# Hybrid SSD and differential-attention layer: the skip path moved into the attention stage, two kinds of DMA moved to ScalarE's queue

## The chip, the cores and the metric

The kernel runs on one core of a Trainium2 chip. The metric is the device time of one execution in microseconds (us). Three runs of the kernel before gave 1235.99, 1236.02 and 1239.23 us, median 1236.02 us. The trace comes from one further execution, under the hardware profiler.

Engines: PE is TensorE's matmul, PEld its weight load, DVE is VectorE, ACT ScalarE, POOL GpSimd, SP SyncE, which here only issues DMAs. Each engine works through its own queue in order.

## The reference, cut to what matters

One encoder layer on 1024 tokens of width 1024. The input is normalised once; that result feeds the layer and, scaled by alpha, also the skip sum at the end.

```python
h = layer_norm(x, ln_emb_g, ln_emb_b)
proj = h @ w_in                      # 1024 x 6688
z, xbc, dt_f, dt_b, q, k, v, g = split(proj)
xbc = silu(centred_dwconv(xbc, conv_w, conv_b))
y = bidirectional_ssd(xs, dt_f, dt_b, Bm, Cm, ...)      # 16 heads, chunks of 128
y_ssm = rms_norm(y * silu(z), ssm_norm_g)
# 8 heads, two softmax maps each, distance penalty
o = (softmax(q1 k1) - lam * softmax(q2 k2)) @ v
y_attn = rms_norm(o, subln_g) * (1 - lam_init) * silu(g)
mix = concat([y_ssm, y_attn]) @ w_out
return layer_norm(ALPHA * h + mix, ln_g, ln_b)
```

## The kernel before, in words

**Arithmetic.** Matmuls run in fp32r. To keep fp32 accuracy, each operand is split into a rounded high part and a low remainder, and a product takes three matmuls (high by high, high by low, low by high). The high part is a cast on ACT, the low part a subtraction on POOL or DVE.

**Stages.** (1) Up to about 60 us: x is loaded, normalised, transposed and split (`h_hi`, `h_lo`). (2) To about 434 us: 52 column blocks of `w_in` begin to be projected (the lane `fill`, weights staged by `weights` in tiles `wst`, split into `whi` and `wlo`), and the two SSD groups run beside them. (3) About 434 to 1085 us: attention, eight heads after each other, eight blocks of 128 queries each, 64 blocks in all. The remaining projections of the next head fill PE between the attention steps. (4) From about 975 us, overlapping the last head: the output projection by `w_out`, then the skip sum and the last layer norm, row block by row block.

**One attention block.** PE computes two score maps into `sc`. DVE adds the distance term and takes the row minimum (tiles `p`, one custom instruction each). ACT exponentiates each (`ACTIVATE p<-p,nm`). DVE forms the two reciprocals `rs`; POOL scales the first map (`TENSOR_SCALAR p<-p,rs`); DVE subtracts the scaled second map from it (`SCALAR_TENSOR_TENSOR p<-p,rs,p`). PE transposes the result (`bk<-ident,p`), ACT and DVE split the transposes into `wh` and `wl`, and PE multiplies by the values every second block. At most two blocks are between scores and transposes.

**What sets the order.** The lanes are Python generators. A planner (`Loom`, lines 47 to 127) emits them into the program in the order of a model of engine times; `LANES` (line 29) holds each lane's rank and margin. PE's instructions, and those issued through `VO` and `AO`, are pinned in that order. Everything else (most of DVE and ACT, all of POOL and SP) is ordered once more by the tile framework's scheduler when the program is built: it may move an instruction ahead of others of its engine if its data and its buffer allow it. On the chip, each engine runs the order that comes out of this.

**DMAs.** All are issued by SP (`dma`, line 250). An SP instruction that waits (for a buffer to be free or for data to be ready) holds up all that stand behind it. The z block's tail (line 478) stores the gated `zs` to DRAM in 16 pieces; `proj_k` (line 921) copies each half of the keys to the other 64 partitions, four DMAs a head. Every DMA's completion counts on one of eight semaphores, given out in turn.

**The skip path.** The lane `residuals` (lines 1189 to 1219) runs in stage 4, once the pool `ow` is open (line 1292). It loads the embedding gain and bias, broadcast to all partitions (`g_e`, `b_e`), scales both by alpha on ACT, and then, for each of the eight row blocks in two halves (tiles `xr`, 128 x 512): a load of x, the normalisation on ACT (line 1213), the multiplication by the gain and the addition of the bias on POOL. The output projection's accumulators (PSUM banks `bk`) are freed by DVE's addition of a bank to `xr` (lines 1225, 1280).

Of the kernel before, what the change touches and what calls it, by code (L numbers as in the profile page):

```python
# [9 lines left out]
F32 = mybir.dt.float32  # L10
# [4 lines left out]
ALU = mybir.AluOpType  # L15
# [10 lines left out]
EPS = 1e-5  # L26
ALPHA = 2.0 ** 0.25

LANES = dict(weights=(0, 0.8), channels=(1, 1.2), steps=(2, 1.6), z_tail=(2, 0.8), conv=(3, 1), v_tail=(3, 0.4), states=(4.4, 0.8), diag=(4.125, 0.6), maps=(4.4, 0.6), gate=(4.375, 0.2), finish=(4.2, 2), scores=(4, 0.8), combine=(4.125, 0.6), values=(4.25, 0.4), fill=(9, 0.8), rows_out=(9, 0.2), y_out=(9, 3), residuals=(9, 2), project_out=(9, 2))


def col_bcast(ap, n):
# [184 lines left out]
def hybrid_layer_kernel(  # L217
# [13 lines left out]
    VO = Engine(loom, nc.vector, "DVE", _dve_cost, pinned=True)  # L231
    AO = Engine(loom, nc.scalar, "ACT", _act_cost, pinned=True)
    SP = Engine(loom, nc.sync, "DMA", _dma_cost)
    x, out = x[0], out[0]
    w_in, w_out, conv_w = w_in[0], w_out[0], conv_w[0]

# [12 lines left out]

    def dma(dst, src):  # L250
        SP.dma_start(dst, src)

    def transpose(dst, src, n=128):
        T.transpose(dst, src, ident[:n, :n])
# [109 lines left out]
    y_dram = [dr.tile([128, 16, 128], F32, name=f"yd{k}") for k in range(8)]  # L364
    acs_dr = [dr.tile([16, NCH, 128], F32, name=f"acs_d{d}") for d in range(2)]
    zd = [dr.tile([NCH, 128, 512], F32, name=f"zd{g}") for g in range(2)]


    g0x = px.enter_context(ExitStack())
# [96 lines left out]
    def z_block(g, j, when=None):  # L466
        def evac(half, ps):
            zr = late["sq"].tile([128, 512], F32, name="zr", bufs=2)
            A.copy(zr, ps)

            def tail():
                pt = bank((128, 4, 128))
                yield (zr, pt)
                for i in range(4):
                    transpose(pt[:, i, :], zr[:, 128 * i:128 * i + 128])
                zs = late["sq"].tile([128, 4, 128], F32, name="zs", tag="zr", bufs=2)
                A.activation(zs, pt, AF.Silu)
                dma(zd[g][4 * half:4 * half + 4, :, 128 * j:128 * j + 128].rearrange("c p n -> p c n"), zs)
                G[g].z_done += 1
            loom.add(tail(), "z_tail")  # L480
        queue.append(Block(Z0 + 512 * g + 128 * j, evac, when))
# [427 lines left out]
    def proj_k(h):  # L909
        H = heads_[h]  # L910

        def evac(half, ps):
            if half == 0:
                H.kk = H.pool().tile([128, 2, S], F32R, name="kk")
                H.kl = H.pool().tile([128, S], F32R, name="kl")
            t = slice(512 * half, 512 * half + 512)
            for m in range(2):
                a, b = slice(64 * m, 64 * m + 64), slice(64 - 64 * m, 128 - 64 * m)
                A.copy(H.kk[a, m, t], ps[a])
                V.tensor_sub(H.kl[a, t], ps[a], H.kk[a, m, t].bitcast(F32))  # L920
                dma(H.kk[b, m, t].bitcast(F32), H.kk[a, m, t].bitcast(F32))
            H.k += 1
        queue.append(Block(K0 + 128 * h, evac, free_since(h, "scored", 8)))

# [176 lines left out]
    for h in range(1, 8):  # L1101
        project_head(h)
    queue[-2].pair = queue[-1].last = True
    for lane in (scores, combine, values):
        loom.add(lane())


# [74 lines left out]
                parts.append((hi, lo))  # L1182
            ahead[tb, part] = parts

    res = {}
    used = set()
    halves = [slice(0, 512), slice(512, 1024)]

    def residuals():

        yield lambda: "pool" in res
        for n, src in (("g", ln_emb_g), ("b", ln_emb_b)):
            res[n] = res["pool"].tile([128, D], F32, name=n + "_e")
            dma(res[n], src.partition_broadcast(128))
            A.activation(res[n], res[n], AF.Copy, scale=ALPHA)
        late = [("zr", 2), ("zr", 2), ("o", 2), ("o", 2), ("osq", 1), ("msq", 1)]
        for tb in range(8):
            yield lambda: tb < len(used) + 2 or tb > NE
            if tb == NE:
                yield lambda: last.v == 2  # L1200
            if tb > NE:
                yield lambda: last.done == 2
            xr = []
            nmr = ap.tile([128, 1], F32, name="nmr", bufs=2)
            V.scalar_tensor_tensor(nmr, mv[tb][:, 0:1], -1.0, rstd[tb], op0=ALU.mult, op1=ALU.mult)
            for n, t in enumerate(halves):
                if tb < NE:
                    xr.append(res["pool"].tile([128, 512], F32, name=f"xr{tb}_{n}"))
                else:
                    tag, bufs = late[2 * (tb - NE) + n]  # L1210
                    xr.append(ap.tile([128, 512], F32, name="xr", tag=tag, bufs=bufs))
                dma(xr[n], x[128 * tb:128 * tb + 128, t])
                A.activation(xr[n], xr[n], AF.Identity, scale=rstd[tb], bias=nmr)
                P.tensor_mul(xr[n], xr[n], res["g"][:, t])
                P.tensor_add(xr[n], xr[n], res["b"][:, t])
            res[tb] = xr
        for n, src in (("g", ln_g[0]), ("b", ln_b[0])):
            res[n + "o"] = res["pool"].tile([128, D], F32, name=n + "_o", tag=n + "_e")
            dma(res[n + "o"], src.partition_broadcast(128))

    def norm_out(tb, xr, po, final):
        st = ap.tile([128, 2, 6], F32, name="bst", bufs=2)
# [95 lines left out]
```

## Time and profile before

| | |
|---|---|
| median of three runs | 1236.02 us |
| the profiled execution | 1237.79 us |
| its span, first to last instruction | 1236.1 us |
| PE busy | 1177.5 us (95%) |
| DVE busy | 903.5 us (73%) |
| ACT busy | 702.8 us (57%) |
| POOL busy | 472.6 us (38%) |
| mean granted TensorE clock | 0.989 |

The shares are means over stages with different limits: PE's idle time, 58.6 us of the span, lies before 60 us (16.2 us of it), in the SSD stage, in some places of stage 4 and after 1200 us (7.7 us), and hardly any in the attention stage. So the rows below are taken stage by stage. A row of the timeline merges equal instructions that follow each other; in brackets stands the idle time of the engine before it and who ended it.

### The profile page before, as it was taken

To read this page: it belongs to the slowest core of one execution; us is meant where nothing else is said; L and a number is where in the kernel's file an instruction comes from. 1 tells how busy PE (TensorE), PEld (TensorE's weight loads), DVE (VectorE), ACT (ScalarE), POOL (GpSimd) and SP (SyncE) were. 2 spreads that over 40 slices of the span, in tenths; PEclk is the share of its full clock that TensorE was granted. 3 is DMA by queue.
4 is the path that set the end of the run, shared out by engine and by line. 5 is a ranking of instruction groups with operands and counts; after the bars stand their busy time and mean duration, and the time that the engine had idled before them with its cause. 6 is when DMAs were issued, how large, how long until landed. Compare 5 with 4: busy or idle time off the path is not lost. (4 is left out here: it accounts for less than half of the span.)

```text
span 1236.1 us, 16491 instructions
## 1 busy us (share of the span) xinstructions
PE 1177.5 (95%) x5881; PEld 923.5 (75%) x5881; DVE 903.5 (73%) x1303; ACT 702.8 (57%) x1281; POOL 472.6 (38%) x404
## 2 busy tenths in 40 slices
PE   5999999899989999999999999999999998999997
PEld 3777667788667777778787777878778776778885
DVE  6686876767875568788788887887878889952334
ACT  4557478734468456565655657556655686641221
POOL 7412564322753223323232333233232429541354
PEclk9999999999999999999999999999999999989999
DMA  6113236522345521011111121121111262233221
GB/s 198 34 32 116 81 110 173 181 65 53 99 118 149 151 63 43 26 46 50 26 48 39 43 53 26 34 52 36 43 36 42 86 225 83 74 103 114 77 86 60
DMA packets 107592, 98.04 MB, mean 79 GB/s; under 512 B 9364, under 2 KB 79349, under 8 KB 107509
## 3 DMA queue, kind: packets, MB, share of 16 engines
q1 hardware_dynamic: 107509, 96.98, 27.4%
q8 instruction: 46, 0.75, 0.3%
q14 instruction: 37, 0.30, 0.1%
HBM read 75.85 MB, written 16.91 MB: 75 GB/s over the span
## 5 line engine op out<-in xcount | busy, mean ns | idle before, releaser
L140 PE MATMUL bk<-hh,whi 128*128 128x512 f32 x832 | 353.8, 425 | 1.3 <-DVE yt L140 0.7
L140 PE MATMUL bk<-hl,whi 128*128 128x512 f32 x832 | 328.1, 394 | 3.3 <-POOL hl L140 3.0
L140 PE MATMUL bk<-hh,wlo 128*128 128x512 f32 x832 | 328.9, 395 | 0.0
L140 POOL TENSOR_TENSOR wlo<-wst,whi 128x512 fp32r<-128x512 f32 x104 | 160.4, 1546 | 145.1 <-ACT whi L140 129.0
L140 ACT ACTIVATE p<-p,nm 128x1024 f32<-128x1024 f32 x128 | 146.8, 1148 | 121.3 <-DVE nm L140 120.6
L140 POOL TENSOR_SCALAR p<-p,rs 128x1024 f32<-128x1024 f32 x56 | 64.5, 1152 | 350.1 <-DVE rs L140 300.4
L140 PEld LDWEIGHTS bk<-hh,whi 128*128 128x128 f32 x832 | 158.3, 190 | 33.8 <-issue 5.7
L140 PEld LDWEIGHTS bk<-hh,wlo 128*128 128x128 f32 x832 | 157.2, 189 | 35.3
L140 PEld LDWEIGHTS bk<-hl,whi 128*128 128x128 f32 x832 | 158.3, 190 | 33.2 <-POOL hl L140 5.5
L140 DVE CUSTOM_DVE_ANT_0 p<-sc,dist 128x1024 f32<-128x1024 f32 x128 | 151.3, 1217 | 11.9 <-PE sc L140 11.2
L140 DVE SCALAR_TENSOR_TENSOR p<-p,rs,p 128x1024 f32<-128x1024 f32 x64 | 127.8, 1997 | 22.6 <-POOL p L140 18.0
L140 DVE TENSOR_TENSOR wl<-bk,wh 128x512 fp32r<-128x512 f32 x128 | 86.9, 683 | 16.1 <-ACT wh L140 14.2
L140 ACT CAST wh<-bk 128x512 fp32r<-128x512 f32 x128 | 74.1, 579 | 43.1 <-PE bk L140 42.4
L140 ACT CAST whi<-wst 128x512 fp32r<-128x512 f32 x104 | 64.0, 621 | 44.4 <-PE bk L140 37.5
L140 PE MATMUL bk<-ident,p 128*128 128x128 f32 x512 | 79.9, 279 | 4.7 <-DVE wl L140 3.0
L140 PEld LDWEIGHTS bk<-ident,p 128*128 128x128 f32 x512 | 61.9, 142 | 29.5 <-DVE wl L140 6.5
L140 ACT ACT_TABLE_LOAD x46 | 59.0, 1283 | 27.9 <-DVE t L140 17.2
L140 PE MATMUL bk<-wh,vh 128*128 128x256 f32 x256 | 74.6, 291 | 0.0
L140 PE MATMUL bk<-wl,vh 128*128 128x256 f32 x256 | 72.2, 282 | 0.9 <-DVE wl L140 0.9
L140 PE MATMUL sc<-kk,q 128*128 128x512 f32 x256 | 72.4, 394 | 0.0
L140 PE MATMUL bk<-wh,vl 128*128 128x256 f32 x256 | 72.0, 281 | 0.0
L140 PEld LDWEIGHTS bk<-xt,t 128*128 128x128 f32 x256 | 44.9, 189 | 24.3 <-issue 15.8
(217 smaller groups left out, 2168.3 us busy)
## 6 DMA issues: line engine op xcount, KB each, us to landing
wst<-in_w_in_dram SPq DMA_DIRECT2D x104, 256.0 KB, 3.0
t<-acs_d SPq DMA_DIRECT2D x64, 256.0 KB, 3.4
ws<-in_w_out_dram SPq DMA_DIRECT2D x32, 256.0 KB, 3.1
ys<-yd SPq DMA_DIRECT2D x32, 256.0 KB, 3.1
xb<-in_x_dram SPq DMA_DIRECT2D x8, 512.0 KB, 6.3
zd<-zs SPq DMA_DIRECT2D x16, 256.0 KB, 3.0
gz<-zd SPq DMA_DIRECT2D x16, 256.0 KB, 3.1
yd<-ys SPq DMA_DIRECT2D x16, 256.0 KB, 2.5
```

Source lines behind the costliest of these rows:

```text
L140: r = f(*args, **kw)
```

## The change

Three edits go together.

(1) **A new lane `skip_rows`**, with rank 9 and margin 2 in `LANES`, starts with the attention lanes. It loads `g_e` and `b_e`, and for each of 16 half row blocks loads x into a tile `xe` (two buffers), normalises it on ACT, multiplies and adds on POOL, and stores it to DRAM (`xr_dram`). `residuals` then only loads `xr` from there. The last gain and bias (`g_o`, `b_o`) are loaded in `skip_rows` too.

(2) **`dma_act`**: the 16 z stores and the 32 key copies are issued by ACT in place of SP.

(3) The DMA scratch is set to 1024 bytes, which leaves room in SBUF for the new tiles.

```diff
+    AD = Engine(loom, nc.scalar, "DMA", _dma_cost)
...
+    def dma_act(dst, src):
+
+        AD.dma_start(dst, src)
...
+    xr_dram = [dr.tile([128, D], F32, name=f"xrd{b}") for b in range(NCH)]
...
-                dma(zd[g][4 * half:4 * half + 4, :, 128 * j:128 * j + 128].rearrange("c p n -> p c n"), zs)
+                dma_act(zd[g][4 * half:4 * half + 4, :, 128 * j:128 * j + 128].rearrange("c p n -> p c n"), zs)
...
-                dma(H.kk[b, m, t].bitcast(F32), H.kk[a, m, t].bitcast(F32))
+                dma_act(H.kk[b, m, t].bitcast(F32), H.kk[a, m, t].bitcast(F32))
...
-    for lane in (scores, combine, values):
+    resid = {}
+
+    def skip_rows():
+
+        for n, src in (("g", ln_emb_g), ("b", ln_emb_b)):
+            resid[n] = ap.tile([128, D], F32, name=n + "_e")
+            dma(resid[n], src.partition_broadcast(128))
+        yield lambda: count["s"] > 1
+        for n in "gb":
+            A.activation(resid[n], resid[n], AF.Copy, scale=ALPHA)
+        left = []
+
+        def store():
+            dst, t = left.pop(0)
+            dma(dst, t)
+
+        for i in range(16):
+            tb, t = i // 2, slice(512 * (i % 2), 512 * (i % 2) + 512)
+            yield lambda: count["s"] >= 3 * i + 3
+            if len(left) > 1:
+                store()
+            xe = ap.tile([128, 512], F32, name="xe", bufs=2)
+            dma(xe, x[128 * tb:128 * tb + 128, t])
+            nmr = ap.tile([128, 1], F32, name="nmr", bufs=2)
+            V.scalar_tensor_tensor(nmr, mv[tb][:, 0:1], -1.0, rstd[tb], op0=ALU.mult, op1=ALU.mult)
+            A.activation(xe, xe, AF.Identity, scale=rstd[tb], bias=nmr)
+            P.tensor_mul(xe, xe, resid["g"][:, t])
+            P.tensor_add(xe, xe, resid["b"][:, t])
+            left.append((xr_dram[tb][:, t], xe))
+        yield lambda: count["s"] >= 54
+        while left:
+            store()
+        for n, src in (("g", ln_g[0]), ("b", ln_b[0])):
+            res[n + "o"] = ap.tile([128, D], F32, name=n + "_o", tag=n + "_e")
+            dma(res[n + "o"], src.partition_broadcast(128))
+
+    res = {}
+    for lane in (scores, combine, values, skip_rows):
         loom.add(lane())
...
         yield lambda: "pool" in res
-        for n, src in (("g", ln_emb_g), ("b", ln_emb_b)):
-            res[n] = res["pool"].tile([128, D], F32, name=n + "_e")
-            dma(res[n], src.partition_broadcast(128))
-            A.activation(res[n], res[n], AF.Copy, scale=ALPHA)
...
-                dma(xr[n], x[128 * tb:128 * tb + 128, t])
-                A.activation(xr[n], xr[n], AF.Identity, scale=rstd[tb], bias=nmr)
-                P.tensor_mul(xr[n], xr[n], res["g"][:, t])
-                P.tensor_add(xr[n], xr[n], res["b"][:, t])
+                dma(xr[n], xr_dram[tb][:, t])
             res[tb] = xr
...
-    nc = _bacc.Bacc("TRN2", target_bir_lowering=False, num_devices=1)
+    nc = _bacc.Bacc("TRN2", target_bir_lowering=False, num_devices=1,
+                     dynamic_dma_scratch_size=1024)
```

PE's order is the same up to the last head and differs there in where the output projection's groups stand among the steps of attention. The orders of the other engines change where the new instructions go. The condition `count["s"] >= 3 * i + 3` spreads the 16 pieces over 48 blocks in the planner's order, but the built program has them in the first ten blocks of attention. The tiles `xe` are named below by their buffer numbers: the first to the last are 9200, 9207, 9215, 9223, 9231, 9239, 9247, 9255, 9263, 9271, 9279, 9287, 9295, 9303, 9311 and 9319; the text numbers them 0 to 15 and calls the blocks of attention b0, b1, and so on.

**POOL, from b3 to b4 of the first head.** `p0` is the first map of a block (p0_4001 and p0_4009 are b3, p0_4106 and p0_4114 are b4). Before:

```order
L140 TENSOR_SCALAR p0_4001<-p0_4001,rs_4069 128x1024
L140 TENSOR_TENSOR wlo_4151<-wst_4067,whi_4150 128x512
L140 TENSOR_SCALAR p0_4106<-p0_4106,rs_4177 128x1024
L140 TENSOR_SCALAR p0_4171<-p0_4171,rs_4246 128x1024
L140 TENSOR_TENSOR o_4011<-o_4011,gate_3823 128x512
```

and now:

```order
L140 TENSOR_SCALAR p0_4009<-p0_4009,rs_4077 128x1024
L140 TENSOR_TENSOR xe_9247<-xe_9247,g_e_9194 128x512
L140 TENSOR_TENSOR xe_9247<-xe_9247,b_e_9196 128x512
L140 TENSOR_TENSOR wlo_4159<-wst_4075,whi_4158 128x512
L140 TENSOR_TENSOR xe_9255<-xe_9255,g_e_9194 128x512
L140 TENSOR_TENSOR xe_9255<-xe_9255,b_e_9196 128x512
L140 TENSOR_TENSOR xe_9263<-xe_9263,g_e_9194 128x512
L140 TENSOR_TENSOR xe_9263<-xe_9263,b_e_9196 128x512
L140 TENSOR_SCALAR p0_4114<-p0_4114,rs_4185 128x1024
```

Between the scaling of b3 and that of b4, POOL now multiplies and adds three tiles `xe`.

**ACT, around the exponentials of b4 and b5 of the first head** (`ACTIVATE p0,ls` and `p1,ls`; p0_4106 and p0_4114 are b4, p0_4171 and p0_4179 b5). Before:

```order
L140 CAST wh_4039<-bk_4112 128x4x128
L140 ACTIVATE p0_4106,ls_4095<-p0_4106,nm_4094 128x1024
L140 ACTIVATE p1_4109,ls_4095<-p1_4109,nm_4094 128x1024
L140 CAST wh_4039<-bk_4125 128x4x128
L140 CAST kk_4134<-bk_4061 64x512 x2
L140 ACTIVATE p0_4171,ls_4156<-p0_4171,nm_4155 128x1024
```

and now:

```order
L140 CAST wh_4047<-bk_4120 128x4x128
L140 ACTIVATE xe_9263<-xe_9263,nmr_9265,rstd4_96 128x512
L140 ACTIVATE p0_4114,ls_4103<-p0_4114,nm_4102 128x1024
L140 ACTIVATE p1_4117,ls_4103<-p1_4117,nm_4102 128x1024
L140 CAST wh_4047<-bk_4133 128x4x128
L140 CAST kk_4142<-bk_4069 64x512
L140 ACTIVATE xe_9271<-xe_9271,nmr_9273,rstd4_96 128x512
L140 DMA kk_4142<-kk_4142 64x512
L140 CAST kk_4142<-bk_4069 64x512
L140 DMA kk_4142<-kk_4142 64x512
L140 ACTIVATE xe_9279<-xe_9279,nmr_9281,rstd5_97 128x512
L140 ACTIVATE p0_4179,ls_4164<-p0_4179,nm_4163 128x1024
```

Tile 8 (9263) stands ahead of b4's exponentials, tile 10 (9279) ahead of b5's, and the key copies stand in ACT's queue.

**SP, in the same stretch.** `wst` are weights of the projections, `xe<-in_x_dram` the loads and `xrd` the stores of the skip rows. Before:

```order
L140 DMA wst_4065<-in_w_in_dram 128x4x128
L140 DMA wst_4067<-in_w_in_dram 128x4x128
L140 DMA wst_4254<-in_w_in_dram 128x4x128
L140 DMA wst_4256<-in_w_in_dram 128x4x128
L140 DMA kk_4134<-kk_4134 64x512 x2
```

and now:

```order
L140 DMA xrd3_147<-xe_9247 128x512
L140 DMA wst_4264<-in_w_in_dram 128x4x128
L140 DMA xe_9263<-in_x_dram 128x512
L140 DMA xrd3_147<-xe_9255 128x512
L140 DMA xe_9271<-in_x_dram 128x512
L140 DMA xrd4_148<-xe_9263 128x512
L140 DMA xe_9279<-in_x_dram 128x512
L140 DMA xrd4_148<-xe_9271 128x512
L140 DMA xe_9287<-in_x_dram 128x512
```

With two buffers, each load of a tile waits for the end of the store that empties its buffer: 9263 for that of 9247, 9279 for that of 9263.

## Rows read from the trace of the kernel before

**Rows 1.** Busy time by stretch: length, PE, PEld, DVE, ACT, POOL, clock, DMA share, GB/s

```profile
600.00:800.00 200.00, 199.21 (x1072) 157.50 (x1071) 161.93 (x239) 122.69 (x213) 61.17 (x45) 1.00 0.16 40
...
```

**Rows 2.** The same view, in the last head and the last stage

```profile
1026.00:1036.00 10.00, 6.04 (x21) 4.90 (x22) 8.96 (x10) 9.16 (x15) 9.92 (x7) 0.83 0.23 71
...
1083.00:1092.00 9.00, 6.13 (x20) 4.73 (x19) 5.67 (x9) 5.04 (x9) 4.11 (x3) 0.64 0.34 106
...
```

**Rows 3.** Timeline of PE in the last head: start, us, instruction, idle time before

```profile
1029.96 0.51 PE L140 MATMUL bk<-oh,oyh 128*128 128x512 f32 x1 [3.98 <-DVE xr L140]
...
1032.26 1.20 PE L140 MATMUL bk<-oh,oyh 128*128 128x512 f32 x2
...
1035.11 0.62 PE L140 MATMUL bk<-ol,oyh 128*128 128x512 f32 x2
...
1086.29 1.11 PE L140 MATMUL bk<-ident,p 128*128 128x128 f32 x4 [2.87 <-DVE wl L140]
```

**Rows 4.** The chain that ended last: start us, us, what

```profile
1078.59 4.24 DMA xr<-in_x_dram
...
1082.93 0.04 ACT xr L140
...
1172.22 56.08 PE bk L140 x240
```

**Rows 5.** Instructions on the tiles xr: count, ns min/median/max, first and last start

```profile
L140 ACT ACTIVATE xr<-xr,nmr,rstd x16: 797/812/818, 1019.7 to 1122.2; 128x512 f32<-128x512 f32 x16
L140 POOL TENSOR_TENSOR xr<-xr,g_e x16: 1267/1296/2288, 1020.6 to 1123.1; 128x512 f32<-128x512 f32 x16
L140 POOL TENSOR_TENSOR xr<-xr,b_e x16: 1267/1454/2279, 1022.0 to 1124.4; 128x512 f32<-128x512 f32 x16
```

**Rows 6.** Timelines of SP and ACT at the start of attention

```profile
435.65 1.28 SPq L140 DMA_DIRECT2D ws<-in_w_out_dram  x3
...
439.46 0.56 ACT L140 COPY gate<-bk 128x512 f32<-128x512 f32 x1
...
```

**Rows 7.** DMA issues: count, KB each, median us from issue to landing

```profile
g_e<-in_ln_emb_g_dram SPq DMA_DIRECT2D x1, 512.0 KB, 4.0
xr<-in_x_dram SPq DMA_DIRECT2D x2, 256.0 KB, 2.7
out_dram<-xr SPq DMA_DIRECT2D x16, 256.0 KB, 2.5
```

**Rows 8.** Timeline of ACT: the first exponentials of b4 and b5

```profile
471.67 1.15 ACT L140 ACTIVATE p<-p,nm 128x1024 f32<-128x1024 f32 x1
...
479.12 1.15 ACT L140 ACTIVATE p<-p,nm 128x1024 f32<-128x1024 f32 x1 [2.66 <-DVE nm L140]
```

**Rows 9.** Timeline of DVE: the subtractions of b4 and b5

```profile
475.76 1.27 DVE L140 SCALAR_TENSOR_TENSOR p<-p,rs,p 128x1024 f32<-128x1024 f32 x1
...
485.13 2.31 DVE L140 SCALAR_TENSOR_TENSOR p<-p,rs,p 128x1024 f32<-128x1024 f32 x1
```

**Rows 10.** Timeline of PE: the first transposes of b4 and b5

```profile
479.99 0.60 PE L140 MATMUL bk<-ident,p 128*128 128x128 f32 x4
...
488.69 0.66 PE L140 MATMUL bk<-ident,p 128*128 128x128 f32 x4
```

**Rows 11.** Timeline of POOL beside b5's subtraction

```profile
484.62 3.97 POOL L140 TENSOR_TENSOR wlo<-wst,whi 128x512 fp32r<-128x512 f32 x2
```

**Rows 12.** What SP's queue waited for: us in total, times, longest

```profile
SPq L140 <- ACT kk L140: 62.4, 16, 7.9
...
SPq L140 <- ACT zs L140: 27.8, 10, 7.2
```

**Rows 13.** SP's issues of the z stores and key copies: ns min/median/max

```profile
L140 SPq DMA_DIRECT2D zd<-zs x16: 359/370/508, 122.2 to 392.2; - x16
...
L140 SPq DMA_DIRECT2D kk<-kk x32: 461/467/1127, 409.6 to 967.7; - x32
```

**Rows 14.** What PE waited for in the SSD stage, 60 to 200 us

```profile
PE bk L140 <- DVE t L140: 2.9, 3, 1.3
...
```

More of the change, by code (lines that the diff above doesn't have):

```diff
@@ L27 @@
 ALPHA = 2.0 ** 0.25
-LANES = dict(weights=(0, 0.8), channels=(1, 1.2), steps=(2, 1.6), z_tail=(2, 0.8), conv=(3, 1), v_tail=(3, 0.4), states=(4.4, 0.8), diag=(4.125, 0.6), maps=(4.4, 0.6), gate=(4.375, 0.2), finish=(4.2, 2), scores=(4, 0.8), combine=(4.125, 0.6), values=(4.25, 0.4), fill=(9, 0.8), rows_out=(9, 0.2), y_out=(9, 3), residuals=(9, 2), project_out=(9, 2))
+LANES = dict(weights=(0, 0.8), channels=(1, 1.2), steps=(2, 1.6), z_tail=(2, 0.8), conv=(3, 1), v_tail=(3, 0.4), states=(4.4, 0.8), diag=(4.125, 0.6), maps=(4.4, 0.6), gate=(4.375, 0.2), finish=(4.2, 2), skip_rows=(9, 2), scores=(4, 0.8), combine=(4.125, 0.6), values=(4.25, 0.4), fill=(9, 0.8), rows_out=(9, 0.2), y_out=(9, 3), residuals=(9, 2), project_out=(9, 2))
 def col_bcast(ap, n):
@@ L1183, in y_out @@
             ahead[tb, part] = parts
-    res = {}
     used = set()
@@ L1203, in residuals @@
             xr = []
-            nmr = ap.tile([128, 1], F32, name="nmr", bufs=2)
-            V.scalar_tensor_tensor(nmr, mv[tb][:, 0:1], -1.0, rstd[tb], op0=ALU.mult, op1=ALU.mult)
             for n, t in enumerate(halves):
@@ L1211, in residuals @@
                     xr.append(ap.tile([128, 512], F32, name="xr", tag=tag, bufs=bufs))
-                dma(xr[n], x[128 * tb:128 * tb + 128, t])
-                A.activation(xr[n], xr[n], AF.Identity, scale=rstd[tb], bias=nmr)
-                P.tensor_mul(xr[n], xr[n], res["g"][:, t])
-                P.tensor_add(xr[n], xr[n], res["b"][:, t])
+                dma(xr[n], xr_dram[tb][:, t])
             res[tb] = xr
-        for n, src in (("g", ln_g[0]), ("b", ln_b[0])):
-            res[n + "o"] = res["pool"].tile([128, D], F32, name=n + "_o", tag=n + "_e")
-            dma(res[n + "o"], src.partition_broadcast(128))
     def norm_out(tb, xr, po, final):
```

## Prediction

> **What bounds the kernel now.** I first read the busy time by stretch. In the middle of attention PE is busy for 199.21 of 200 us at full clock [rows 1]: there PE is the bound, and whatever makes PE wait is lost. In the last head it is not. From 1026 to 1036 us PE works for 6.04 of 10 us at a mean clock of 0.83, from 1083 to 1092 us for 6.13 of 9 us at 0.64 [rows 2]. PE's timeline shows the two places: 3.98 us until DVE has added to `xr`, and 2.87 us until DVE has made `wl` [rows 3]. After a gap PE is slow for a while: a pair of matmuls takes 1.20 us at 1032.26 and 0.62 us at 1035.11 [rows 3]. That is the lower of the clock's two levels, 1.2 for 2.4 GHz, after an idle PE.
>
> Then I read the chain of waits. The second gap leads back to a load of `xr`, 4.24 us from issue to landing, for which ACT stood; ACT's activation followed within 0.1 us of the landing (1078.59 + 4.24 = 1082.83, start 1082.93), with the casts queued behind it. The chain ends with PE working through from 1172.22 for 56.08 us [rows 4], as it does from the second gap on. So a microsecond saved before 1086 us is a microsecond of the result.
>
> **Part 1: the skip path leaves the last stage.** It removes there 16 activations of 0.81 us and 32 POOL instructions of about 1.30 and 1.45 us (medians) [rows 5], between 1019.7 and 1124.4 us. POOL is busy for 9.92 of 10 us where PE first waits [rows 2], because it makes `xr`. Now `xr` needs only a load, which no longer stands behind the loads of `g_e` and `b_e`. Both gaps hang on this path: 3.98 + 2.87 = 6.85 us. The clock gives back about (1 - 0.83) x 10 = 1.7 us after the first. After the second (1 - 0.64) x 9 = 3.2 us, less half of the 2.87 us idle, if that time counts at the low level already: 1.8 us. Together 10.3 us. Both ends: 4 us, if only the first gap closes and the rest is late for something else (DVE is at 8.96 of 10 us in that stretch [rows 2]), and 12 us, if DVE's instructions get shorter beside an idle POOL too. I take 8.5 us, nearer to the sum of the rows, less a little for what is late next: the casts of the weight rows on ACT.
>
> **Part 2: the skip path enters attention.** As work it is cheap: ACT and POOL are busy for 123 and 61 of 200 us there [rows 1]. But it enters at fixed places of queues that run in order, and it hangs on a ring of two buffers. One turn of a buffer is a load of 2.7 us [rows 7], an activation of 0.81 us, a multiplication and an addition of 1.30 + 1.45 us [rows 5], and a store of 2.5 us, taken from the stores of the result, which have the same size [rows 7]: 8.8 us. With five handovers of 0.1 us, as the one above [rows 4], it is 9.3 us. Two tiles come out in each turn.
>
> The start: SP is free of the last stage's stores at 435.65 us; there `g_e` is issued, which lands after 4.0 us, at 439.65 [rows 6, 7]. ACT is done with its copy at 439.46 + 0.56 = 440.0 us [rows 6] and scales `g_e` and `b_e`, each as large as a map of 1.15 us [rows 8]: 442.3 us. I let tile 0 be loaded by then.
>
> In ACT's new order tile 8 stands ahead of the exponentials of b4. It is four turns behind tile 0: 442.3 + 4 x 9.3 + 0.8 = 480.3 us. Those exponentials started at 471.67 us [rows 8], so they come 8.6 us late. Tile 10 stands ahead of b5: 442.3 + 5 x 9.3 + 0.8 = 489.6 us for 479.12, 10.5 us late. PE has some slack: the subtraction of b4 ended at 475.76 + 1.27 = 477.03 and its transposes began at 479.99, 2.96 us later; for b5 it is 485.13 + 2.31 = 487.44 and 488.69, 1.25 us [rows 9, 10]. So PE stalls for about 8.6 - 2.96 = 5.6 us at b4, and by b5 is 10.5 - 1.25 = 9.2 us late in all. The slow clock after b4's stall lies under the wait for b5; that after b5 costs 1.7 us, as in part 1. After b5 the delay itself gives the ring time, since tiles 11 to 15 are spread over four blocks. Sum: 11 us.
>
> Both ends: at POOL's shortest instructions (1.27 us each) and no handovers a turn is 8.5 us, b5 is 6.5 us late and PE loses about 5 us; if loads or stores are also faster than their medians here, 2 us. At a load of 4.24 us, as in the chain [rows 4], a turn is 10.9 us, and PE loses 442.3 + 54.5 + 0.8 - 479.12 - 1.25 + 1.7, about 19 us. A gain is excluded: nothing here is taken from any engine that attention waits for.
>
> POOL and DVE also hinder each other. The same subtraction on DVE takes 1.27 us while POOL is idle, and 2.31 us beside POOL's `wlo`, two of which took 3.97 us [rows 9, 11] for 1.3 us each otherwise. By these rows each added POOL instruction costs DVE or POOL up to 1.04 us, 33 us for 32, if all of them meet such an instruction. I charge none of it in the sum, because DVE waits in the stretch in which the ring is late. The Trainium skill ("SBUF — State Buffer", section "SBUF: two separate sides") says why: a DVE instruction with two SBUF inputs and a GpSimd instruction that reads SBUF take the shared ports in turn, each for its whole length. The trace agrees, with 2.31 against 1.27 us. By that rule every added POOL instruction that meets such a DVE instruction lengthens the turn itself, which makes it a rival below.
>
> **Part 3: the DMAs on ACT.** ACT gets 16 issues of 0.37 us and 32 of 0.47 us [rows 13], 21 us in all, in some 850 us. A key copy waits for the cast ahead of it on ACT itself; behind it stand the exponentials of the next block, which waited for DVE for 2.66 us anyway [rows 8]. That idle time hides two issues, and without it each pair would cost up to 0.9 us a head. SP no longer waits 62.4 us for casts of keys and 27.8 us for `zs` [rows 12]. In attention this frees weight loads that PE doesn't wait for. In the SSD stage the loads of the decay rows `t` stand behind the z stores, and PE waits for DVE on `t` 2.9 us between 60 and 200 us [rows 14]. A DMA on ACT also waits for an earlier DMA on the same semaphore, often one of SP's; that could hold ACT up. Ends: 3 us gained, 3 us lost, about the 2.9 us either way. I take 0.5 us gained. The smaller scratch and the earlier loads of `g_o` and `b_o` cost nothing that a row shows.
>
> **The sum.** -8.5 + 11 - 0.5 = +2.0 us. The profiled execution took 1237.79 us, so 1239.8 us in its terms; the median of the runs is 1.8 us below it, so 1238.0 us. A measurement of this kernel tells 0.3%, 3.7 us, from no change: faster is below 1232.3, slower above 1239.7.
>
> **The rivals.**
> *The ring keeps up.* If a turn takes little over 7 us, tile 10 is ready at 442.3 + 35 + 0.8 = 478.1, before b5 needs it. PE then loses 2 us at most, and the time is 1236.0 - 8.5 + 2 - 0.5 = 1229 us. For it: PE hardly waits in attention [rows 1], and small transfers in a quiet stretch may beat their medians. Against it: 2.7 + 2.5 us of transfers and 3.6 us of work leave nothing to save but the rounding. Chance 0.30.
> *The ring is much slower.* If POOL's instructions meet DVE's and take over 2.2 us (their maxima are 2.29 and 2.28 [rows 5]), or loads take 4.24 us, a turn is nearly 11 us and attention loses 19 us: 1236.0 - 8.5 + 19 - 0.5 = 1246 us. It decides from a turn of some 10 us on. This is where the rule on the shared ports would lead. For it: SP's queue holds loads of weights between the tiles, which wait for POOL as well. Against it: DMA is at 0.16 of its time in attention [rows 1]. Chance 0.15.
> *The gain at the end does not come.* The gaps close but others open, since DVE was at 9 tenths there: 4 us gained instead of 8.5, and 1242.5 us. For it: PE's order changes only there. Against it: POOL's load goes, and with it DVE's longer instructions. Chance 0.15.
>
> **How the numbers follow.** The forecast has 0.40, with its own range of 1234 to 1243 us: 0.02 of it is faster, 0.25 the same, 0.13 slower. The ring that keeps up: 0.30 faster. The slow ring: 0.15 slower. The missing gain: 0.13 slower, 0.02 same. Together 0.32 faster, 0.27 same, 0.41 slower. The range reaches to the centre of the first rival, less 2 us, and past that of the second: 1227 to 1250 us.
>
> **What would show it.** In the profile after, PE should be idle for 5 to 12 us between 440 and 520 us, with b4's and b5's transposes waiting, and ACT waiting for the DMA of `xe` ahead of the exponentials; stores of one tile 9 to 10 us after those of the tile two before. In the last head no wait on `xr` ahead of PE, and POOL idle around 1030 us. The prediction is wrong if PE stays at 99% through b4 and b5, or if the last head still has gaps of several us. Part 3 is wrong if ACT waits for a DMA ahead of its own DMA issues.

## The result

The changed kernel took 1247.36 us (median of four runs, 1244.69 to 1248.30) against 1236.01 us: 1.0085 of the time before, 95% interval 1.0059 to 1.0110, about 10.5 us slower by this ratio (the two medians differ by 11.4 us). The forecast was 1238 us with a range of 1227 to 1250 us, and slower the likeliest of the three outcomes. So the side and the range hold, but the middle is 9 us off. Two terms of the sum were mis-sized, and the third was a gain and a loss that nearly cancel.

In its trace the changed kernel's span is 1246.1 us, 10.0 us more than before. The start times of the first exponentials on ACT divide the span into four parts:

| us | before | changed | |
|---|---|---|---|
| to the first exponentials of attention | 437.17 | 436.97 | -0.2 |
| from there to the second head's | 73.49 | 92.59 | +19.1 |
| from there to the last head's | 480.80 | 477.49 | -3.3 |
| from there to the end | 244.64 | 239.05 | -5.6 |

**The first head.** The busy times by stretch of the changed kernel, with the columns of [rows 1, 2]:

```profile
434.00:600.00 166.00, 151.36 (x783) 118.17 (x782) 124.79 (x193) 102.25 (x172) 89.39 (x65) 0.97 0.34 101
...
1036.00:1047.00 11.00, 6.58 (x39) 5.50 (x40) 9.84 (x18) 6.62 (x11) 1.30 (x1) 0.94 0.54 169
1042.00:1052.00 10.00, 6.03 (x16) 4.67 (x17) 5.15 (x9) 3.47 (x7) 0.00 (x0) 0.68 0.30 102
```

PE is idle for 14.6 us of the first 166 us of attention, and its clock falls there (0.97); after that it is as busy as in [rows 1] (199.69 of 200 us from 600 to 800 us). The chain of waits of the changed kernel (start, us, what) shows one turn of the ring after the other:

```profile
441.98 0.81 ACT xe L140
...
448.61 3.72 DMA xe<-in_x_dram
...
452.49 0.83 ACT xe L140
...
453.38 1.29 POOL xe L140
...
454.75 2.56 POOL xe L140 x2
...
457.38 1.30 POOL xe L140
458.69 0.34 SPq L140
...
461.83 0.83 ACT xe L140
...
475.75 2.00 DMA xrd<-xe
...
477.82 2.95 DMA xe<-in_x_dram
```

On ACT tile 0 comes at 441.98 us, tiles 2, 4, 6 and 8 at 452.49, 461.83, 472.20 and 480.94 us. Four turns make 38.96 us, 9.74 us each, where 9.3 were forecast (the odd tiles 1 to 9 take 10.5 us a turn), and tile 8 ended the wait for b4's exponentials at 480.9 + 0.8 us, where 480.3 was forecast. ACT's timeline, against [rows 8], with tiles 8 and 10 and the exponentials of b4 and b5:

```profile
480.94 0.82 ACT L140 ACTIVATE xe<-xe,nmr,rstd 128x512 f32<-128x512 f32 x1 [4.39 <-DMA xe<-in_x_dram]
481.66 1.14 ACT L140 ACTIVATE p<-p,nm 128x1024 f32<-128x1024 f32 x1
...
489.74 0.81 ACT L140 ACTIVATE xe<-xe,nmr,rstd 128x512 f32<-128x512 f32 x1 [3.33 <-DMA kk<-kk]
490.46 1.14 ACT L140 ACTIVATE p<-p,nm 128x1024 f32<-128x1024 f32 x1
```

b4 is 10.0 us late and b5 11.3 us (8.6 and 10.5 forecast). The wait ahead of tile 10 is put down to a key copy, but the load of that tile, issued at 486.55 us, landed about then too (the median of these loads is 3.4 us). The way of the first three turns isn't the one that I added up: the load of tile 2 needs only the end of tile 0's store, but it stands behind tile 1's store in SP's queue, and that waits for POOL's second tile. So such a turn holds two tiles on POOL (5.3 us) and one issue in place of one tile and a store's flight. Only the fourth goes by the store (2.00 us from 475.75). The two sums are nearly equal.

What the forecast lacks comes behind b5. PE's timeline in the changed kernel, with its longest wait in the first head and the large one in the last, answers to [rows 3]:

```profile
524.02 1.11 PE L140 MATMUL bk<-ident,vc 128*128 128x128 f32 x4 [4.30 <-ACT vc L140]
...
1046.47 0.80 PE L140 MATMUL bk<-oh,oyh 128*128 128x512 f32 x1 [3.14 <-DVE xr L140]
```

The chain of waits leads from the first of them back to tile 15:

```profile
513.84 1.30 POOL wlo L140
515.16 0.38 SPq L140
...
515.58 3.38 DMA xrd<-xe
518.99 2.59 DMA xe<-in_x_dram
...
521.68 0.04 ACT xe L140
...
523.48 0.49 ACT vc L140
```

Tile 13's store stands in SP's queue behind a load of weights (the issue at 515.16) that waits for POOL's `wlo`, itself behind tile 13 on POOL. That adds 1.7 us to the turn, and `vc` stands behind tile 15 on ACT. The exponentials of b6 come 10.8 us late, no more than those of b5; those of b7 13.6 us, and those of the second head's first block 18.9 us.

**The last head.** POOL is free (1.30 of 11 us), and `xr` has long been loaded. But PE still waits 3.14 us for DVE's addition to `xr`, at the output projection's `oh`, as in the first gap of [rows 3], and its clock falls to 0.68 afterwards. DVE is busy for 9.84 of these 11 us. Its addition stands behind a subtraction that waits for ACT's scaling of the first map: in the last head that scaling is on ACT, not on POOL, in both kernels. DVE's timeline before

```profile
1027.47 1.84 DVE L140 SCALAR_TENSOR_TENSOR p<-p,rs,p 128x1024 f32<-128x1024 f32 x1 [0.58 <-ACT p L140]
1029.23 1.27 DVE L140 TENSOR_TENSOR xr<-xr,bk 128x512 f32<-128x512 f32 x2
```

and now:

```profile
1043.93 1.28 DVE L140 SCALAR_TENSOR_TENSOR p<-p,rs,p 128x1024 f32<-128x1024 f32 x1 [1.02 <-ACT p L140]
...
1045.74 1.28 DVE L140 TENSOR_TENSOR xr<-xr,bk 128x512 f32<-128x512 f32 x2
```

Before, ACT's scaling stood behind three activations of `xr` (2.23 us from 1024.17); POOL had the second `xr` tile ready at 1028.23 us, a microsecond ahead of the addition. Only the second gap is gone.

### The profile page after: what moved, and what is told of

Read it like the earlier page. It is cut to its first block, busy times and chain, and to the rows that moved or that the text cites. A ratio compares the mean times of both kernels' runs of the same rounds, so it can differ in the third digit from the quotient of the medians.

```text
span 1246.1 us, 16518 instructions
## 1 busy us (share of the span) xinstructions
PE 1175.3 (94%) x5881; PEld 924.2 (74%) x5881; DVE 899.1 (72%) x1311; ACT 705.5 (57%) x1281; POOL 473.5 (38%) x404
## 4 chain that ended last, share of the span: by engine, by line
PE 56%; DVE 18%; ACT 8%; DMA 6%; POOL 4%; issue 4%; SPq 0%; ACTq 0%; DVEq 0%; POOLq 0%
PE bk L140 44%; PE sc L140 9%; DVE p L140 5%; ACT p L140 4%; PE sb L140 3%; DVE yt L140 2%; DMA gz<-zd 2%; DVE xc L140 2%; POOL xe L140 2%; DVE t L140 1%; DMA xe<-in_x_dram 1%; POOL p L140 1%; DVE osl L140 1%; ACT t L140 1%; DVE wl L140 1%
## 5 line engine op out<-in xcount | busy, mean ns | idle before, releaser
L140 POOL TENSOR_TENSOR wlo<-wst,whi 128x512 fp32r<-128x512 f32 x104 | 164.7, 1588 | 126.6 <-ACT whi L140 113.1
L140 DVE SCALAR_TENSOR_TENSOR p<-p,rs,p 128x1024 f32<-128x1024 f32 x64 | 119.1, 1861 | 19.5 <-POOL p L140 13.4
```

The lines of the kernel that those rows point to most:

```text
L140: r = f(*args, **kw)
```

## The experiments

Ratios are to the kernel before in the same batch. The parts are those of the table above, one trace each.

| kernel | median us | ratio, 95% interval | to attention | first head | heads 2 to 7 | to the end |
|---|---|---|---|---|---|---|
| before, again | 1234.12 | 0.9997, 0.9983 to 1.0011 | 434.80 | 73.48 | 481.45 | 240.97 |
| skip path alone | 1254.61 | 1.0166, 1.0152 to 1.0180 | 434.84 | 94.66 | 481.53 | 238.27 |
| both kinds of DMA alone | 1232.78 | 0.9984, 0.9970 to 0.9997 | 435.06 | 72.88 | 477.67 | 241.09 |
| key copies alone | 1230.04 | 0.9966, 0.9955 to 0.9978 | 437.76 | 72.87 | 477.43 | 241.74 |
| z stores alone | 1239.81 | 1.0036, 1.0022 to 1.0051 | 439.06 | 73.51 | 481.66 | 242.57 |
| no skip work | 1230.01 | 0.9960, 0.9948 to 0.9972 | 438.31 | 72.87 | 478.03 | 238.09 |
| no POOL work | 1236.29 | 1.0009, 0.9995 to 1.0022 | 438.37 | 79.78 | 477.89 | 239.26 |
| four buffers | 1244.05 | 1.0076, 1.0053 to 1.0098 | 436.61 | 88.93 | 477.41 | 239.05 |
| first eleven tiles | 1242.70 | 1.0058, 1.0042 to 1.0075 | 437.48 | 85.34 | 478.18 | 238.10 |
| spread | 1233.23 | 0.9986, 0.9974 to 0.9997 | 439.32 | 74.40 | 478.87 | 239.51 |
| spread, scaling on POOL | 1229.79 | 0.9958, 0.9943 to 0.9973 | 438.12 | 74.36 | 479.08 | 236.94 |
| the same, z stores on SP | 1226.08 | 0.9920, 0.9907 to 0.9933 | 437.74 | 74.41 | 479.11 | 236.64 |

**The kernel before, again** (no edit).

> The kernel before once more, unchanged, for a second trace of it: how far the stages vary from one execution to the next. Expected: 1235 us; attention from the first exponentials to those of the last head within 0.5 us of the 554.3 us of the first trace; the 434 us ahead of it within 2 us; the last stage within 2 us of 244.6 us.

The first head agrees within 0.01 us, the heads after it within 0.7. The part ahead of attention varies by 2.4 us, the last by 3.7 us; about half of the last is the clock, as told below under the hardware. So a difference of a microsecond in the middle parts counts in a single trace, in the outer ones not.

**The skip path alone.**

```diff
-                dma_act(zd[g][4 * half:4 * half + 4, :, 128 * j:128 * j + 128].rearrange("c p n -> p c n"), zs)
+                dma(zd[g][4 * half:4 * half + 4, :, 128 * j:128 * j + 128].rearrange("c p n -> p c n"), zs)
...
-                dma_act(H.kk[b, m, t].bitcast(F32), H.kk[a, m, t].bitcast(F32))
+                dma(H.kk[b, m, t].bitcast(F32), H.kk[a, m, t].bitcast(F32))
```

> The changed kernel with the z stores and the key copies back on SP; the skip path in attention stays. Theory A (the two-buffer ring of `xe`, one turn about 9.6 us, holds ACT's exponentials up by about 19 us in the first head and a half; the DMAs on ACT are worth the 3.3 us by which the lag falls from head 1 to head 7): the 19 us stay and the 3.3 us go, so 1247.4 + 3.3 = about 1251 us, and ACT waits for `xe` loads as long as in the changed kernel (17 us between 434 and 530 us). Theory B (the key copies in ACT's queue, one of which stands between two tiles `xe`, make a good part of the loss): ACT waits less, the loss falls by 5 us or more, 1242 us or less.

**Both kinds of DMA alone**: the kernel before with the two lines above on ACT.

> The kernel before with only the z stores and the key copies moved to ACT's queue (and the smaller DMA scratch); the skip path stays in the last stage. Theory A: the lag against the kernel before falls by about 0.5 us in each of heads 1 to 6, and the first 434 us are the same within 0.5 us: 1236.0 - 3.3 = about 1232.7 us. Theory B: ACT is held up by its own DMA issues and their waits: slower than before, 1239 us or more. If the fall of the lag has another cause (the slowed start of attention itself gives it back), the time is that of before, 1236 us.

Theory B falls: without key copies on ACT the first head is 94.66 us long, no shorter than 92.59. Theory A holds for the heads: the 3.3 us by which the changed kernel gains from head 2 on are there with the moved DMAs and no skip path (477.67) and not there without them (481.53). The total of the moved DMAs alone is smaller than the forecast 3.3 us, so something takes part of it back.

**No skip work**: in `skip_rows` only the loads of `g_o` and `b_o` stay.

```diff
-                dma(xr[n], xr_dram[tb][:, t])
+                dma(xr[n], x[128 * tb:128 * tb + 128, t])
```

> The changed kernel without the skip path's computation: nothing is loaded, normalised, scaled or stored for it in attention, and the last stage adds x itself (the normalisation, the gain and the bias of the skip sum are left out). Theory A: only the 19 us of attention go: 1247.4 - 19 = about 1228 us, and the last head gains about 5.5 us against before. Rival: part of the 19 us was there only because it was given back later (the lag falls by 3 us through heads 1 to 6); then the time is about 1231 us. If attention's loss comes from the moved DMAs, 1240 us.

0.9960 against 1.0085: the skip rows in attention cost 1.25%, 15.4 us by the runs, and 92.59 - 72.87 = 19.7 us of the first head by the traces. The two traced spans differ by 18.8 us; why the ratios give less stays open. Without that work PE is idle for 0.4 of 166 us:

```profile
434.00:600.00 166.00, 165.60 (x894) 131.76 (x893) 131.34 (x199) 101.59 (x176) 50.26 (x37) 1.00 0.19 49
```

**The tiles spread over 48 blocks.**

```diff
-    ... skip_rows=(9, 2), ...
+    ... skip_rows=(8.9, 2), ...
...
-            A.activation(resid[n], resid[n], AF.Copy, scale=ALPHA)
+            AO.activation(resid[n], resid[n], AF.Copy, scale=ALPHA)
...
-            A.activation(xe, xe, AF.Identity, scale=rstd[tb], bias=nmr)
+            AO.activation(xe, xe, AF.Identity, scale=rstd[tb], bias=nmr)
```

> The changed kernel with the lane of the skip rows one rank ahead of the projections' lane in the planner, and with its activations on ACT (the scaling of gain and bias, and the tiles `xe`) held in the planner's order: the 16 tiles now stand ahead of the exponentials of blocks 2, 6, 8, 12 and so on to 48, with two buffers as before. Theory A: each tile has 20 to 40 us for a turn of 9.6 us, ACT waits for none of them, and attention loses nothing: about 1228 us. Theory C (each added POOL instruction lengthens DVE's or its own by up to 1.04 us, wherever it stands, or its loads and stores slow others): a loss of up to 10 us spread over six heads stays, about 1236 us.

It needs both edits. At rank 9 the lane stands behind `fill`, which has the same rank and is added earlier, so the planner emits all 16 tiles only in the last head; their numbers, 9200 to 9319, lie between those of that head's b0 and b4 (p0_9014 and p0_9668). What the section on the change says of the planner's order is wrong in this: the condition on `count["s"]` spreads nothing. And the rank alone, of which there is no run, gives a built program with the same order on every engine as the changed kernel, because the scheduler moves ready work ahead. With both, the first head is 74.40 us and the others 478.87: 2.4 us more than with no skip work, and no wait of PE over 0.6 us there but one of 1.2 us that the kernel before has too (1.0). Theory A holds; theory C is left with these 2.4 us. The time, 1233 us, is 5 us above the forecast 1228, which took all 19 us off. In the traces the heads give back 16.8 us, and the part ahead of attention is 2.4 us longer, by which single traces of it vary.

**No POOL work**: the multiplication and the addition of each tile are left out.

```diff
             A.activation(xe, xe, AF.Identity, scale=rstd[tb], bias=nmr)
-            P.tensor_mul(xe, xe, resid["g"][:, t])
-            P.tensor_add(xe, xe, resid["b"][:, t])
```

> The changed kernel without the two POOL instructions on each tile `xe` (the gain and the bias of the skip sum are left out); loads, the normalisation on ACT and stores stay, with two buffers. The order of ACT is nearly the same (tiles 6 to 9 ahead of the exponentials of b4, 10 and 11 ahead of b5's). Theory A (the turn of the ring sets the loss): a turn falls from 9.6 to about 2.7 + 0.8 + 2.5 + 0.4 = 6.4 us; tile 8 comes at 442.3 + 4 x 6.4 + 0.8 = 468.7 us, before b4 needs ACT at 471.7, and tile 10 at 475.1 for 479.1: PE loses 2 us at most between 440 and 530 us, and the time is about 1231 us. Rival (the transfers, 4 MB each way within 90 us, or the mere presence of the tiles in ACT's queue): 10 us or more of the loss stay, 1240 us or above.

A middle case: 79.78 us in the first head, 12.8 us less than the changed kernel, but 6.9 more than with no skip work. ACT's timeline, with tiles 8 and 9 and b4:

```profile
475.35 0.81 ACT L140 ACTIVATE xe<-xe,nmr,rstd 128x512 f32<-128x512 f32 x1 [1.16 <-DMA xe<-in_x_dram]
478.26 0.82 ACT L140 ACTIVATE xe<-xe,nmr,rstd 128x512 f32<-128x512 f32 x1 [2.10 <-DMA xe<-in_x_dram]
...
479.58 1.15 ACT L140 ACTIVATE p<-p,nm 128x1024 f32<-128x1024 f32 x1
```

Tile 8 comes at 475.35 instead of 468.7: four turns of 7.95 us from tile 0 (443.54), not 6.4. And tile 9, which I left out of account, holds b4 up until 479.1. A turn without POOL still holds a load of 3.4 us (the median of `xe` in the changed kernel; I had taken 2.7) and the work that ACT does ahead of the tile. So POOL's two instructions make two thirds of the loss; neither theory had the other third.

**Four buffers.**

```diff
-            if len(left) > 1:
+            if len(left) > 3:
...
-            xe = ap.tile([128, 512], F32, name="xe", bufs=2)
+            xe = ap.tile([128, 512], F32, name="xe", bufs=4)
...
-                     dynamic_dma_scratch_size=1024)
+                     dynamic_dma_scratch_size=512)
```

> The changed kernel with four buffers for the tiles `xe` instead of two (and a DMA scratch of 512 bytes, so that they fit). Theory A (the ring of two alone): four tiles in a turn of 9.6 us, tile 8 ready by about 442 + 2 x 9.6 = 461 us, PE loses under 3 us, about 1231 us. Theory D (POOL is the next bound, and the scheduler only pulls the tiles further ahead): with four buffers tile 11 stands ahead of b4's exponentials instead of tile 8. POOL takes 2 x 1.3 us for each of the eight tiles that must be done before tile 11 can be loaded, and some 4 us of its own in each of the four blocks: 442.9 + 21 + 16 = 480 us, and with a store, a load and an activation 486 us for 471.7: b4 comes 14 us late, and the time stays within 5 us of the changed kernel's 1247 us.

Theory D holds: the first head is 88.93 us, only 3.7 us shorter. ACT's timeline with tile 11 and b4, and POOL's share of the stretch ahead (fifth busy time):

```profile
481.19 0.81 ACT L140 ACTIVATE xe<-xe,nmr,rstd 128x512 f32<-128x512 f32 x1 [5.43 <-DMA xe<-in_x_dram]
...
482.50 1.15 ACT L140 ACTIVATE p<-p,nm 128x1024 f32<-128x1024 f32 x1
```

```profile
452.50:492.50 40.00, 29.27 (x154) 21.53 (x152) 31.79 (x49) 26.27 (x45) 39.06 (x31) 0.99 0.55 174
```

POOL works for 39.06 of 40 us (29.31 in the changed kernel). A longer ring alone doesn't help: the scheduler fills it with more tiles ahead of the same block.

**The first eleven tiles.**

```diff
-    ... skip_rows=(9, 2), ...
+    ... skip_rows=(8.9, 2), ...
...
-            A.activation(xe, xe, AF.Identity, scale=rstd[tb], bias=nmr)
+            (A if i < 11 else AO).activation(xe, xe, AF.Identity, scale=rstd[tb], bias=nmr)
```

> The changed kernel with tiles 0 to 10 where they are and tiles 11 to 15 held in the planner's order (ahead of the exponentials of blocks 36, 38, 42, 44 and 48). If the loss up to b5 is all of the first eleven tiles and the rest belongs to tiles 11 to 15: the exponentials of b5 come 11 us later than in the kernel before, as in the changed kernel, and those of the next head's b0 still only 11 to 12 us later instead of 18.9: 1247.4 - 7 = about 1240 us. If the late part is the after-effect of the first stall (the in-order queues catching up), whichever tiles follow: b0 of the next head is about 19 us late, and the time is that of the changed kernel, 1247 us.

ACT's timeline has b5 at 490.35 us and the second head's b0 at 522.82:

```profile
490.35 1.14 ACT L140 ACTIVATE p<-p,nm 128x1024 f32<-128x1024 f32 x1
...
522.82 1.15 ACT L140 ACTIVATE p<-p,nm 128x1024 f32<-128x1024 f32 x1
```

11.2 and 12.2 us after the kernel before. So the loss up to b5 belongs to the first eleven tiles, and 92.59 - 85.34 = 7.3 us to tiles 11 to 15. The traced spans, 1246.1 and 1239.1 us, agree with that; the ratios don't quite: 1.0085 becomes 1.0058, 3.3 us, and the forecast 1240 us lies just below the four runs (1240.28 to 1245.08). The trace is of one of the two faster ones (1240.84), and what makes the others slower stays open.

**The last head's scaling on POOL.** The spread version, with one line for all heads:

```diff
-            if H is heads_[7]:
-                A.activation(p0, p0, AF.Copy, scale=rs[:, 0:1])
-            else:
-                P.tensor_scalar(p0, p0, rs[:, 0:1], 1.0, op0=ALU.mult, op1=ALU.mult)
+            P.tensor_scalar(p0, p0, rs[:, 0:1], 1.0, op0=ALU.mult, op1=ALU.mult)
```

> The version with the tiles spread over 48 blocks, and in the last head the scaling of the first map on POOL as in the other heads, instead of on ACT: eight activations of 1.15 us leave ACT, which works for 49 of 85 us in the last head and stands ahead of the output projection's casts, and go to POOL, which is busy for 12 of these 85 us. If ACT's queue is what is late in the last head: 2 to 3 us faster than the spread version, about 1231 us. If DVE is (9.84 of 11 us busy where PE waits 3.14 us in the changed kernel), no difference, 1233 us; DVE's subtractions could get longer beside POOL, 1235 us.

0.9986 becomes 0.9958. The wait of PE for `xr` from 960 us on (us in total, times, longest), in the spread version

```profile
PE bk L140 <- DVE xr L140: 3.4, 2, 3.1
```

and with the scaling on POOL, where the longest wait is now another:

```profile
PE bk L140 <- DVE osl L140: 2.0, 1, 2.0
...
PE bk L140 <- DVE xr L140: 0.7, 1, 0.7
```

The wait for `xr` is down to 0.7 us: from 1024 to 1046 us PE is busy for 22.00 of 22 us at clock 1.00, in the spread version for 17.56 at 0.84. DVE's addition to `xr` had stood behind a subtraction that waited for ACT's scaling. The slow clock is not gone, though. It has moved ahead, behind the waits of 2.0 us for `osl` and 1.3 us for `wl`, to a stretch that the spread version runs at 1.00:

```profile
1009.00:1016.00 7.00, 5.93 (x16) 3.96 (x17) 3.29 (x5) 6.06 (x8) 2.07 (x2) 0.52 0.77 220
```

So what this version gains is the shorter waiting (2.5 us in the last part).

**The z stores alone** (the kernel before with that line on ACT) and **on SP again** (in the version with the scaling on POOL).

> The kernel before with only the z stores moved to ACT (and the smaller DMA scratch). By the traces so far: 2 us slower than before, ratio 1.0015, with PE waiting about 8 us for `t` ahead of 434 us, and no fall of the lag through the heads. If the z stores cost nothing: the same as before, within its interval, and PE waits 3.5 to 5 us for `t`.

> Spread tiles, the first map scaled on POOL in the last head too, and the z stores back on SP, so that only the key copies are on ACT. In the seven traces with the z stores on ACT the first exponentials of attention started at 435.1 to 439.3 us, mean 437.5, in the three with them on SP at 434.8 to 437.2, mean 435.6, and PE waited 7.7 to 9.1 us for the decay rows `t` instead of 3.5 to 5.1 us. If the z stores on ACT cause it: about 2 us faster than the same version with them on ACT, 0.995 - 0.0015 = 0.994 of the kernel before, about 1227.5 us, and PE waits about 4 us for `t`. If that is chance: 1229.8 us as before.

Both point one way: +0.36% with them on ACT, -0.38% (0.9958 to 0.9920) without. PE's waits ahead of 434 us, with the z stores alone on ACT

```profile
PE bk L140 <- DVE t L140: 7.8, 6, 2.7
PE sb L140 <- DVE H L140: 5.8, 6, 2.7
```

and with them on SP, in the last version:

```profile
PE sb L140 <- DVE H L140: 8.1, 7, 2.7
PE bk L140 <- DVE t L140: 5.2, 4, 2.1
```

All nine traces with the z stores on ACT have 7.7 to 9.1 us at `t`, the five with them on SP 3.5 to 5.2. But most of that is given back at `H`, the state of the SSD: 4.1 to 5.9 us in the nine, 6.6 to 8.1 in the five. All of PE's waits ahead of 434 us come to 23.6 us on average in the nine and 22.4 in the five, and attention starts at 437.7 and 436.5 us. So the traces place some 1.2 us of the 4.5; the rest I can't place, and why DVE gets to `t` later stays open. The smaller DMA scratch has no run of its own, but the first of these two comparisons has it on one side only and the second on both, and they agree but for the sign; so it costs nothing that these runs show. The last version, 1226.08 us, is the fastest: 0.8% below the kernel before, 1.6% below the changed one.

**The key copies alone** (the kernel before with that line on ACT).

> The kernel before with only the key copies moved to ACT (and the smaller DMA scratch). By the fall of the lag from head to head (0.5 us a head, 3.4 us in all): ratio 0.997, about 1231.6 us. By the ratios of the two kernels with the moves done together and with the z stores alone (0.9984 - 1.0036): -0.5%, about 1229 us; then some 3 us of it lie outside the heads, and the trace should show them ahead of 434 us or in the last stage. If the copies on ACT cost as much as they give: 1235 us.

-0.34%, 4.2 us. Heads 2 to 7 take 477.43 us, 3.4 us less than in the kernel before. PE does not gain them at its weights: from start to start of its instructions, the two traces differ in these heads by 2.3 us at the transposes of `vc`, by 1.2 us at the matmuls by `osl`, which DVE makes for the norm, and by 0.1 us in the sum of all the rest. PE's timeline in the second head, at the first transposes of `vc`, before and now:

```profile
575.41 0.39 PE L140 MATMUL bk<-hh,wlo 128*128 128x512 f32 x1
575.91 0.66 PE L140 MATMUL bk<-ident,vc 128*128 128x128 f32 x4
```

```profile
575.34 0.39 PE L140 MATMUL bk<-hh,wlo 128*128 128x512 f32 x1
575.57 0.60 PE L140 MATMUL bk<-ident,vc 128*128 128x128 f32 x4
```

ACT's copy of `vc` just ahead, before and now:

```profile
575.29 0.57 ACT L140 COPY vc<-bk 128x512 f32<-128x512 f32 x1
```

```profile
573.75 0.58 ACT L140 COPY vc<-bk 128x512 f32<-128x512 f32 x1
```

And DVE, before and now:

```profile
569.81 1.42 DVE L140 TENSOR_TENSOR msq<-msq,rt 128x512 f32<-128x512 f32 x2
571.26 1.22 DVE L140 CUSTOM_DVE_ANT_0 p<-sc,dist 128x1024 f32<-128x1024 f32 x1
```

```profile
569.73 1.22 DVE L140 CUSTOM_DVE_ANT_0 p<-sc,dist 128x1024 f32<-128x1024 f32 x1
...
572.02 0.69 DVE L140 TENSOR_TENSOR msq<-msq,rt 128x512 f32<-128x512 f32 x1
```

DVE now makes b6's maps ahead of two products of the norm (`msq`), so b6's exponentials and behind them the copy of `vc` come 1.5 us earlier on ACT, and the transposes start 0.23 us after the start of the matmul ahead of them instead of 0.50: the pause is gone. That order is the scheduler's; the traces show it, but no run has this order without the moved copies.

## Why the prediction was right or wrong

**The side was right, and so was the mechanism of part 2.** A ring of two buffers, a turn of 9 to 10 us, tile 8 ahead of b4 and tile 10 ahead of b5 in ACT's queue: the two tiles and the two exponentials came within 1.5 us of the forecast. That the turn came so near is in part luck: three of the four turns went another way than the one added up, and a load took 3.4 us, not 2.7. No skip work and spread tiles show that nothing else of the path costs much.

**Its size was not.** "After b5 the delay itself gives the ring time, since tiles 11 to 15 are spread over four blocks" is the step that failed. 11 us were charged, 19.1 came. The five tiles stand ahead of three blocks, not four: two ahead of b6, two ahead of b7, one ahead of the second head's first. Up to b6 the step held (10.8 us late). Behind it the delay gave the ring nothing, because the turns grew: those of tiles 11 to 15 took 9.5 us (tile 11 to 13, on ACT) to 15.1 us (9 to 11), 11.7 us on average, since key copies, `wlo` and weight loads stand between them in the queues. The eleven-tile version measures it: 11.9 us without the five tiles, 7.3 us more with them. The 19 us stand as the end of that term's range, from a slow load, and as the price of the second rival. That rival needed a turn of nearly 11 us from slow POOL instructions or loads ahead of b5. Such turns came only behind b5, and the loads' median was 3.4 us; that the total met its 1246 us is chance.

**Part 1 was over-sized.** 8.5 us were forecast with a lower end of 4. With the skip path in the last stage that part takes 240.97 to 244.64 us (mean of five traces 242.2), without it 238.09 to 239.51 (mean of the seven with the last head's scaling still on ACT 238.8): 3.4 us. Two things were wrong. The first gap was put down to POOL, which was busy, but by both traces it was DVE's queue behind ACT's scaling, and it came back at 3.14 us, as it does with no skip work at all; that is the third rival, the missing gain, and moving the scaling to POOL shows the cause in the version with spread tiles. By the prediction's own sign ("In the last head no wait on `xr` ahead of PE") this part was wrong, though the time lies in the range. And the gain of the clock after the second gap, 1.8 us, was counted from one execution: the second trace of the same program doesn't have it.

**Part 3 was right in total and wrong in content.** Half a microsecond was forecast, -2.0 us measured for both together, -4.2 and +4.4 for each alone. That PE would feel the z stores at `t`, with "about 2.9 us either way", was right in place, with the sign left open, but PE gets most of it back at `H`. That ACT's issues would be hidden was right. That the key copies are worth something through the order of DVE was not thought of.

**What does not add up.** By the ratios, the skip path alone costs 1.66% and the DMAs alone gain 0.16%, but together they cost 0.85%, not 1.5%: 8 us are missing (5.5 us by the ratios of the medians, 1.0157, 0.9980 and 1.0092). The traces hold 3.2 us of them (spans of 1249.3 and 1246.1 us). The traced run of the skip path alone took 1251.01 us, as theory A had it, and the median is 1254.61; what lies between them stays open.

## What to carry to other kernels

Work that is free by its busy time is not free by its place: if a scheduler may move it ahead, it goes to the first spot where its data is ready, and a short ring of buffers then drags an in-order engine with it. Pin such work to the spot where it is meant to run, before giving it more buffers. And before a gap is credited to the engine that is busy beside it, follow the waiting engine's own queue: take away the work of the supposed cause and see if the gap goes.

## What the runs showed of the hardware

The same program ran at two speeds after the same gap. In the first trace PE stood still for 2.87 us [rows 3] and was then at 0.64 of its clock [rows 2]: partly at the lower of its two levels, 1.2 for 2.4 GHz. In the second trace of the kernel before it stood still for 2.29 us, and the clock stayed at 1.00; pairs of matmuls take 0.62 us there, and took 1.05 in the first. The gap in PE's timeline

```profile
1083.53 0.66 PE L140 MATMUL bk<-ident,p 128*128 128x128 f32 x4 [2.29 <-DVE wl L140]
```

and the busy times of the stretch:

```profile
1080.80:1089.80 9.00, 6.71 (x33) 5.09 (x33) 6.62 (x10) 4.49 (x9) 4.14 (x3) 1.00 0.50 148
```

The gap at `xr`, 3.36 us in that trace, does lower the clock, to 0.70 from 1023 to 1033 us.

So a gap whose length varies by half a microsecond can be worth two or three microseconds, and a second trace of the same kernel shows it. Nor does the length of one gap tell all: with the last head's scaling on POOL the clock fell to 0.52 after gaps of 2.0 and 1.3 us with two matmuls between them.

POOL and DVE met less than feared. In the changed kernel the two groups of added POOL instructions have medians of 1289 and 1292 ns and, over attention, means of 1353 and 1361:

```profile
L140 POOL TENSOR_TENSOR xe<-xe,b_e 128x512 f32<-128x512 f32 x16 | 21.8, 1361 | 1.3
L140 POOL TENSOR_TENSOR xe<-xe,g_e 128x512 f32<-128x512 f32 x16 | 21.6, 1353 | 16.9 <-ACT xe L140 16.9
```

That is 32 x 67 ns = 2.1 us of meetings, where 33 us was the bound. The one at 485.77 us took 2.36 us beside a subtraction of DVE that started at 485.72. The Trainium skill's rule ("SBUF — State Buffer", section "SBUF: two separate sides") that the two lock each other out of a shared port agrees with that instruction. The meetings did not set the turn up to b4, where no POOL instruction on `xe` took over 1.30 us; behind b5 one stands in the chain, tile 13's addition (2.15 us from 511.72), worth 0.9 us.
